# Fixing ScalarE's order in the stick-breaking attention of half 0

## The chip, the cores and the metric

The kernel runs on one core of a Trainium2 chip. A core has five engines with a queue each: TensorE (PE, with its weight loads as PEld), VectorE (DVE), ScalarE (ACT), GpSimd (POOL) and SyncE (SP), which issues nearly all DMAs here. Each engine takes its instructions strictly in order and waits on semaphores for the others. The metric is device time in microseconds for one execution, given as the median of several runs.

## The reference

A decoder layer of width 1024 on 2048 tokens and 16 meta tokens: an RMS norm, one wide input projection, stick-breaking attention (8 heads of 64), sliding-window attention with sinks (16 query heads), two gated branch projections, an output projection and a last norm. The change lies in the stick-breaking part:

```python
z = einsum('bqhd,bkhd->bhqk', q, k) * d ** -0.5
log_beta = log_sigmoid(z)
log_1m = where(mask, log_beta - z, 0.0)
rev = lax.cumsum(log_1m, axis=3, reverse=True)
suffix = concatenate([rev[..., 1:], zeros], axis=-1)
w = where(mask, exp(log_beta + suffix), 0.0)
out = einsum('bhqk,bkhd->bqhd', w, v)
```

With s = sigmoid(-z), the weight of a key is the product of s over all later keys, less that product with the key's own s in it. The kernel keeps the running product and multiplies it with differences of v.

## The kernel before

Tokens stand in reverse order, so the suffix product is a prefix product along a row. They are cut into four groups of 512 (16 blocks of 128); half 0 works on groups 2 and 3, half 1 on groups 0 and 1, and the meta tokens follow group 3 as keys. Matrix operands are split into a high and a low part, and a product is three matmuls (high by high, high by low, low by high).

In each half, projections and sliding-window attention come first, then stick-breaking attention, then more gate projections; a final stage does the branch and output projections. During stick-breaking TensorE alternates between gate projections (`gate`, whose matmuls are on L464 and whose result is taken out on L615) and attention steps. `weave` does that: for each piece of the main work it draws steps from the side generator `stick`, by a ratio of estimated costs.

`stick` goes over 8 heads, and in each over the half's query groups, group 3 first and then group 2. For a group it goes over n = 0 .. 3-g key groups and four rows j of each. A step s does the following.

- `row(h, g, n, j)` for step s: two score matmuls into one or two `ps_z` banks (L918), a sigmoid on ScalarE per bank (L921), and a scan on VectorE that forms the running product (L926 in the diagonal group, with the mask, L928 in the others). In the rows that reach the meta keys (the last n) GpSimd copies the 16 meta columns of the row into `mr` (L934).
- `turn` for the step six earlier (`LT[0]` is 6): up to four TensorE transposes into a `ps_t` bank (L943), then `evac_split`: ScalarE copies the bank out as `wth` (L126) and VectorE forms the remainder `wtl` (L127).
- When that earlier step is in the last key group and has i = 0, `split_meta`: ScalarE copies `mr` into the high half of `m` (L953, the meta copy), VectorE subtracts for the low half (L954, the remainder).
- When it has i = 1, `turn_meta`: TensorE transposes `m` (L959, the meta transpose) and ScalarE copies the result in four parts into `wm` (L963).
- `values` for a step before that: two matmuls with `wth` and `wtl` against v differences (L975); the last of a unit is the meta product with `wm`, after which four ScalarE instructions with a bias (L981) take the result out and DMAs store it.

A unit here is one head and one query group of half 0: 16 units, numbered in the order in which they run, each with one L953, one L954 and one L959. There are two banks each of `ps_g`, `ps_z`, `ps_t` and `ps_o`, 12 row buffers, and two buffers each of `mr` and `m`.

The order on TensorE is the program's own throughout (`manual_schedule` for PE at the top). For the other engines a scheduler of the framework places the instructions by a simulated timeline, except in stretches under `manual_schedule`: the start of the kernel (VectorE, ScalarE, SP) and the gate products after stick-breaking of half 0 (VectorE, ScalarE).

Of the kernel before, what the change touches and what calls it, by code (L numbers as in the profile page):

```python
# [48 lines left out]
def tile_kernel(ctx, tc, x, xt, meta, metat, gain, w_in, w_sb, w_sw, w_out, sinks, fgain,  # L49
# [94 lines left out]
    def weave(main, side, ratio, credit=0.0):  # L144

        for c in main:
            clock[0] += c
            credit = min(credit + c * ratio, 6.0)
            while credit > 0:
                n = next(side, None)  # L150
                if n is None:
                    credit = float("-inf")
                    break
                if n == 0:
                    credit = 0.0
                    break
                credit -= n
        return credit
# [5 lines left out]
    def drain(*gens):  # L164
        for _ in chain(*gens):
            pass
# [319 lines left out]
    def col_tile(w, g, use, first=False, bank="g", mbank="o"):  # L486

        acc = ps(bank)
        pm = None
        yield from gemm(acc, w, g, first)  # L490
        if first:
            pm = ps(mbank)
            gemm_meta(pm, w)
        use(g, acc, None if pm is None else meta_sum(pm))
        yield 0.65
# [125 lines left out]
    def tiles_by_tile(makes, groups, meta=False):  # L621
        for mk in makes:
            w, use, wants = mk()
            for n, g in enumerate(reversed(groups) if wants == "back" else groups):
                yield from lagged(col_tile(w, g, use, meta and wants and n == 0))
# [6 lines left out]
    def lagged(gen):  # L632

        for n, c in enumerate(gen):
            yield c
            if n in (2, 4, 6):
                flush({2: soon, 4: late, 6: pending}[n])
# [713 lines left out]
    for half, groups in enumerate(halves):  # L1351
# [61 lines left out]
        with tc.tile_pool(name=f"sb{half}", bufs=1, side="left") as bp:  # L1413
            hsplit[0] = vsplit[0] = False
            side = stick(groups, bp)
            drain(tiles_by_tile(gts[few:few + 1], groups))
            rest = 28 - FAST - PLAIN if half == 0 else 23
            cost_sb = 8 * sum(4 * (4 - g) for g in groups) * 1.31 + 16 * 0.33 + LT[half] * 0.86
            ratio = cost_sb / ((rest - few - 1) * 10.4)
            weave(tiles_by_tile(gts[few + 1:rest], groups), side, ratio)  # L1420
            if half == 0:
                hsplit[0] = vsplit[0] = True
                plain = [mk() for mk in gts[rest:rest + 2]]
            drain(side)
# [95 lines left out]
```

## Time and profile before

| | us |
|---|---|
| median of 3 runs | 2091.56 |
| lowest and highest run | 2090.66, 2092.18 |
| profiled execution | 2093.26 |
| its span, first to last instruction | 2091.4 |
| stick-breaking of half 0, from the span's start | about 372 to 562 |
| first and last L953 of half 0 | 380.46, 554.48 |

A profile row of a timeline gives start, duration, engine, line, operation, what it writes and reads, and in brackets the idle time of the engine just before it and the instruction that ended that. "Idle before" of a group is the sum over its instructions. A matmul row's duration contains its pipeline: matmuls of 512 columns that follow each other start about 0.23 us apart though each is given 0.39. So a delay of TensorE is read from starts, and from the idle time in brackets. PEclk is the clock that was granted to TensorE, 1.00 being full speed.

### The profile page before, as it was taken

The numbers are of one execution on the slowest core, as the hardware profiler recorded it, in microseconds if no ns is written. First come the engines' busy times: TensorE is split into PE (matmuls) and PEld (weight loads), VectorE is DVE, ScalarE is ACT, GpSimd is POOL, SyncE is SP. The second block draws the span as 40 slices with busy tenths as digits, with TensorE's granted clock in tenths as the row PEclk, the third lists the DMA queues.
The fourth block names the chain that finished last, engine by engine and source line by source line (L and its number), as shares of the span: only waits on it lengthen the run. The fifth ranks groups of instructions, "written<-read, shape, count | busy, mean of one in ns | idle before, by whom it ended". The sixth has DMA issues, their size and how long they took to land. (4 is left out here: it accounts for less than half of the span.)

```text
span 2091.4 us, 30949 instructions
## 1 busy us (share of the span) xinstructions
PE 2076.3 (99%) x10579; PEld 1744.8 (83%) x10579; DVE 1463.0 (70%) x2383; ACT 1091.4 (52%) x2657; POOL 345.7 (17%) x682
## 2 busy tenths in 40 slices
PE   9999999999999999999999999999999999999998
PEld 7888888888888888888888888888888888788887
DVE  7897986877687754887728788777774547464543
ACT  6677774577665335777735555655653212321121
POOL 1233444331000000233310000000000343000000
PEclk9999999999999999999999999999999999999999
DMA  9855555866377574435455344343424987568532
GB/s 338 307 195 201 188 175 179 252 199 185 91 278 298 209 247 163 159 126 177 150 171 161 120 130 129 114 129 98 121 83 165 350 318 223 182 229 305 154 100 91
DMA packets 170093, 391.46 MB, mean 187 GB/s; under 512 B 23728, under 2 KB 28208, under 8 KB 169936
## 3 DMA queue, kind: packets, MB, share of 16 engines
q1 hardware_dynamic: 169648, 389.23, 55.8%
q8 instruction: 83, 1.36, 0.3%
q14 instruction: 74, 0.61, 0.1%
q10 hardware_dynamic: 288, 0.27, 0.0%
HBM read 241.68 MB, written 145.18 MB: 185 GB/s over the span
## 5 line engine op out<-in xcount | busy, mean ns | idle before, releaser
L464 PE MATMUL ps_g<-xh,wh 128*128 128x512 f32 x1264 | 517.0, 409 | 1.1 <-DVE tmp L680 0.6
L464 PE MATMUL ps_g<-xl,wh 128*128 128x512 f32 x1264 | 495.6, 392 | 0.7 <-DVE xl L1199 0.6
L464 PE MATMUL ps_g<-xh,wl 128*128 128x512 f32 x1264 | 495.7, 392 | 0.0
L928 DVE TENSOR_TENSOR_SCAN row<-row 128x512 f32<-128x512 f32 (+4 forms) x256 | 290.1, 1134 | 116.2 <-POOL row L923 60.1
L464 PEld LDWEIGHTS ps_g<-xh,wl 128*128 128x128 f32 x1264 | 237.8, 188 | 52.7
L464 PEld LDWEIGHTS ps_g<-xh,wh 128*128 128x128 f32 x1264 | 238.5, 189 | 39.9 <-ACT xh L1198 1.4
L464 PEld LDWEIGHTS ps_g<-xl,wh 128*128 128x128 f32 x1264 | 239.2, 189 | 38.0 <-DVE xl L1199 1.8
L921 ACT ACTIVATE row<-ps_z 128x512 f32<-128x512 f32 (+4 forms) x352 | 175.1, 509 | 159.3 <-PE ps_z L918 155.0
L126 ACT ACTIVATE wth<-ps_t 128x512 fp32r<-128x512 f32 (+1 forms) x320 | 171.6, 536 | 61.4 <-PE ps_t L943 59.6
L127 DVE SCALAR_TENSOR_TENSOR wtl<-ps_t,wth 128x512 fp32r<-128x512 f32 (+1 forms) x320 | 188.7, 590 | 21.3 <-ACT wth L126 20.7
L918 PE MATMUL ps_z<-kt,q 128*128 128x512 f32 (+4 forms) x704 | 183.7, 349 | 2.0 <-ACT row L921 1.9
L943 PE MATMUL ps_t<-ident,row 128*128 128x128 f32 x1088 | 171.4, 273 | 1.0 <-DVE wtl L127 0.9
L943 PEld LDWEIGHTS ps_t<-ident,row 128*128 128x128 f32 x1088 | 134.5, 140 | 33.1 <-DVE wtl L127 1.8
L918 PEld LDWEIGHTS ps_z<-kt,q 128*128 128x128 f32 x704 | 124.4, 188 | 27.4 <-ACT row L921 5.1
L975 PE MATMUL ps_o<-wth,vc 128*128 128x512 f32 (+1 forms) x320 | 131.2, 410 | 0.0
L975 PE MATMUL ps_o<-wtl,vc 128*128 128x512 f32 (+1 forms) x320 | 116.4, 364 | 0.0
L767 ACT ACTIVATE sc<-sc,nm 128x129 f32<-128x129 f32 x256 | 100.0, 393 | 30.5 <-DVE nm L765 29.5
L934 POOL COPY mr<-row 128x16 f32<-128x16 f32 x128 | 28.4, 224 | 444.2 <-DVE row L928 401.8
L615 ACT ACTIVATE tmp<-ps_g 128x512 f32<-128x512 f32 x80 | 48.0, 600 | 80.5 <-PE ps_g L464 74.3
L299 ACT CAST ringl<-gt 128x512 fp32r<-128x512 f32 x32 | 19.9, 621 | 127.1 <-DVE gt L297 93.3
L117 POOL TENSOR_SCALAR wh<-raw 128x1024 fp32r<-128x1024 f32 (+1 forms) x45 | 49.8, 1108 | 212.7 <-PE ps_g L464 90.3
L123 POOL TENSOR_TENSOR wl<-raw,wh 128x256 fp32r<-128x256 f32 x88 | 83.2, 975 | 2.0
(442 smaller groups left out, 4202.3 us busy)
## 6 DMA issues: line engine op xcount, KB each, us to landing
wh<-h_in_w_in SPq DMA_DIRECT2D x66, 512.0 KB, 3.9
wl<-l_in_w_in SPq DMA_DIRECT2D x66, 512.0 KB, 5.1
h_in_w_in<-wh SPq DMA_DIRECT2D x50, 512.0 KB, 3.3
l_in_w_in<-wl SPq DMA_DIRECT2D x50, 512.0 KB, 4.1
raw<-in_w_in SPq DMA_DIRECT2D x49, 512.0 KB, 5.3
q<-qd SPq DMA_DIRECT2D x128, 128.0 KB, 3.2
vc<-vd SPq DMA_DIRECT2D x48, 256.0 KB, 3.2
kd<-tmp SPq DMA_DIRECT2D x32, 256.0 KB, 3.4
```

The costliest lines, as they stand in the source:

```text
L117: G.tensor_scalar(h, src, 1.0, 1.0, op0=ALU.mult, op1=ALU.mult)
L123: G.tensor_tensor(l[:, c], src[:, c], f32(h[:, c]), op=ALU.subtract)
L126: A.activation(h, acc, AF.Copy, scale=scale)
L127: V.scalar_tensor_tensor(l, acc, scale, f32(h), op0=ALU.mult, op1=ALU.subtract)
L464: T.matmul(acc, lhsT=a[:, k, :], rhs=b[:, k, :], start=k == i == 0, stop=k == KT - 1 and i == 2)
L615: A.activation(e, acc, AF.Sigmoid)
L767: A.activation(sc[:, hh, :], sc[:, hh, :], AF.Exp, bias=nm[:, hh:hh + 1], accum_out=den[:, hh:hh + 1])
L918: T.matmul(z[:, :m], lhsT=qt[:, j * P:(j + 1) * P], rhs=kt[h][:, k0 + c:k0 + c + m], start=t == 0, stop=t == 1)
L921: A.activation(r[:, c:c + m], z[:, :m], AF.Sigmoid, scale=-1.0)
L928: V.tensor_tensor_scan(r[:, :w], r[:, :w], r[:, :w], last[j] if n else 1.0, op0=ALU.mult, op1=ALU.min)
L943: T.transpose(tr[:, j * P:(j + 1) * P], rows_of[h, g, n - (j > i), j][:, k0:k0 + P], ident)
L975: T.matmul(o[:, :n], lhsT=v, rhs=r, start=first and r is wh, stop=last)
```

## The change

While `weave` runs in half 0, ScalarE too is under `manual_schedule`: its instructions stand in the order in which the program records them. GpSimd, VectorE and SP stay with the scheduler, whose timeline is worked out anew.

```diff
             ratio = cost_sb / ((rest - few - 1) * 10.4)
+            order = ExitStack()
+            if half == 0:
+                order.enter_context(tc.manual_schedule(engines={mybir.EngineType.Activation}))
             weave(tiles_by_tile(gts[few + 1:rest], groups), side, ratio)
+            order.close()
             if half == 0:
```

In the built kernels the instructions are the same in number and kind. ScalarE's order differs in the place of the 16 L953 alone, VectorE's in that of the 16 L954. Unit 1 on ScalarE, before and after:

```
before                          after
L921 row (last of the block)    L921 row (last of the block)
L953 m<-mr                      L921 row x3
L921 row x3                     L126 wth<-ps_t
L126 wth<-ps_t                  L615 tmp<-ps_g
L615 tmp<-ps_g                  L953 m<-mr
L921 row                        L921 row
L126 wth<-ps_t                  L126 wth<-ps_t
L963 wm<-ps_o x4                L963 wm<-ps_o x4
```

On VectorE L954 then stands directly behind the L127 that goes with the L126 in front of L953. TensorE's and GpSimd's orders are the same in both, and on SP two neighbouring DMAs have changed places.

## Prediction

> **What bounds the kernel now.** I read the page's busy line first, then the waits of the stage that the change touches, then the groups, then the timeline around single instructions.
>
> ```profile
> span 2091.4 us, 30949 instructions
> PE 2076.3 (99%) x10579; PEld 1744.8 (83%) x10579; DVE 1463.0 (70%) x2383; ACT 1091.4 (52%) x2657; POOL 345.7 (17%) x682
> ```
> TensorE is busy for all but 15.1 of 2091.4 us. So ScalarE's order is worth only what it adds to or takes from TensorE's waits. The half's stick-breaking runs from about 372 to 562 us. Its waits (engine and line that waited, what ended the wait, us in total, times, longest), then its busy times, then two groups (busy us, mean ns, idle time ahead):
>
> ```profile
> ACT m L953 <- POOL mr L934: 6.7, 8, 3.1
> DVE m L954 <- ACT m L953: 4.2, 6, 1.4
> PE ps_z L918 <- ACT row L921: 1.9, 3, 1.2
> ACT row L921 <- PE ps_z L918: 31.5, 60, 1.0
> 372.00:562.00 190.00, 187.62 (x1071) 158.95 (x1070) 149.16 (x213) 132.88 (x364) 42.23 (x89) 1.00 0.62 189
> L953 ACT CAST m<-mr 128x64 fp32r<-128x64 f32 x16 | 3.9, 243 | 6.9 <-POOL mr L934 6.7
> L959 PE MATMUL ps_o<-ident,m 128*128 128x128 f32 x16 | 4.3, 272 | 0.0
> ```
> ScalarE waits 6.7 us at the meta copy L953 and VectorE 4.2 us at the remainder L954 behind it. But TensorE idles only 190.00 - 187.62 = 2.4 us here, and never at the transpose L959, which reads what L953 and L954 wrote. TensorE's clock is 1.00 throughout.
>
> **The change, part by part.** No instruction is added or removed. There are 16 units (8 heads by 2 query groups), each with one L953, one L954 and one L959. The scheduler placed L953 just after the sigmoids of the row block that ends the unit; the program's own place is three steps later, behind the copy-out L126 of the transposes of `turn` with i = 0. L954 follows on VectorE, to just behind the L127 of the same transposes. In program order L959 is one step later on TensorE and does not move. Nothing else moves except one DMA pair on SP's queue: a gate result is now issued ahead of the low half of a weight copy.
>
> ```profile
> 493.33 0.38 SPq L59 DMA_DIRECT2D l_in_w_in<-wl  x1
> 493.83 0.35 SPq L59 DMA_DIRECT2D gs<-tmp  x1
> 494.23 1.08 SPq L59 DMA_DIRECT2D raw<-in_w_in  x1
> 500.07 0.32 SPq L59 DMA_DIRECT2D vc<-vd  x1
> ```
> In the trace SP issues these at 493.33 and 493.83, the load behind them at 494.23 for 1.08 us, and nothing until 500.07. Two issues that change places inside that row of issues cost nothing; the idle 4.8 us cover them, and without that cover it would be one issue, 0.4 us.
>
> **Unit 1** is the one with the long wait (start, us, engine, line):
>
> ```profile
> 379.63 0.39 PE L464 MATMUL ps_g<-xh,wl 128*128 128x512 f32 x1
> 380.46 0.24 ACT L953 CAST m<-mr 128x64 fp32r<-128x64 f32 x1 [3.13 <-POOL mr L934]
> 380.74 0.23 DVE L954 TENSOR_TENSOR m<-mr,m 128x64 fp32r<-128x64 f32 x1 [0.70 <-ACT m L953]
> 381.24 3.46 DVE L926 TENSOR_TENSOR_SCAN row<-row,mask 128x512 f32<-128x512 f32 x3 [0.27 <-ACT row L921]
> 381.25 0.73 PE L918 MATMUL ps_z<-kt,q 128*128 128x512 f32 x2 [1.24 <-ACT row L921]
> 382.96 0.62 PE L918 MATMUL ps_z<-kt,q 128*128 128x512 f32 x2
> 383.64 0.14 PEld L959 LDWEIGHTS ps_o<-ident,m 128*128 128x128 f32 x1
> 383.75 0.27 PE L959 MATMUL ps_o<-ident,m 128*128 128x128 f32 x1
> 384.61 0.67 DVE L127 SCALAR_TENSOR_TENSOR wtl<-ps_t,wth 128x512 fp32r<-128x512 f32 x1
> 385.19 1.21 DVE L926 TENSOR_TENSOR_SCAN row<-row,mask 128x512 f32<-128x512 f32 x1
> 385.33 0.20 PEld L943 LDWEIGHTS ps_t<-ident,row 128*128 128x128 f32 x2 [0.34 <-DVE wtl L127]
> ```
> Today L953 blocks the sigmoids behind it, so the score matmuls wait until 381.25. Without it they could follow the last gate matmul at 379.63 by about 0.23 (matmuls of 512 columns start that far apart): 1.4 us earlier, and 0.1 more because the held pair took 0.73 where a free one takes 0.62. TensorE would then come to L959 at 383.75 - 1.5 = 382.25. VectorE cannot follow so far. The scans before are done 0.70 + 0.23 + 0.27 = 1.2 us before 381.24, at 380.0. Three scans fill the 3.37 us from 381.24 to 384.61, so L127 starts at 380.0 + 3.37 = 383.37 and ends 0.67 later at 384.04. L954 is now behind it.
>
> The step from the end of L127 to L959: the next VectorE instruction starts 0.09 before L127's end (385.19 against 385.28), and L954 lasts 0.23: +0.14. TensorE takes up a result of VectorE 0.05 after its end (385.28 to 385.33). The matmul comes 0.11 behind its weight load (383.64 to 383.75). Together **0.30 us**. So L959 starts at 384.34: a wait of 2.1 us where there was none, and 0.59 later than today. The wait of 0.34 that today comes at 385.33 falls away, since it is for the same L127. Net for unit 1: 0.59 - 0.34 = **+0.25 us**; the gain of 1.5 is given back.
>
> On VectorE's instruction start there is a rule that can be left out of the sum. The Trainium skill, "VectorE: DVE Perf Modes", section "The DRAIN you can't avoid", says the next VectorE operation does not start until the pipeline is empty. By it L954 would begin at L127's end, 0.09 later in each of nine waits, and the total below would be 3.8 in place of 3.0. The rows at 384.61 and 385.19 show an earlier start, so I do not take it.
>
> **Units 2 to 16.** Here TensorE seldom waited, so its place at L959 stays what it is; the new wait is 0.30 plus the time by which L127 ends after that place. Units 2, 3, 8, 9, 14 and 16:
>
> ```profile
> 397.23 0.69 DVE L127 SCALAR_TENSOR_TENSOR wtl<-ps_t,wth 128x512 fp32r<-128x512 f32 x1 [0.42 <-ACT wth L126]
> 397.94 0.27 PE L959 MATMUL ps_o<-ident,m 128*128 128x128 f32 x1
> ...
> 405.51 0.67 DVE L127 SCALAR_TENSOR_TENSOR wtl<-ps_t,wth 128x512 fp32r<-128x512 f32 x1
> 405.93 0.27 PE L959 MATMUL ps_o<-ident,m 128*128 128x128 f32 x1
> ...
> 466.82 0.67 DVE L127 SCALAR_TENSOR_TENSOR wtl<-ps_t,wth 128x512 fp32r<-128x512 f32 x1
> 467.31 0.27 PE L959 MATMUL ps_o<-ident,m 128*128 128x128 f32 x1
> ...
> 474.89 0.66 DVE L127 SCALAR_TENSOR_TENSOR wtl<-ps_t,wth 128x512 fp32r<-128x512 f32 x1
> 475.99 0.27 PE L959 MATMUL ps_o<-ident,m 128*128 128x128 f32 x1
> ...
> 538.27 0.66 DVE L127 SCALAR_TENSOR_TENSOR wtl<-ps_t,wth 128x512 fp32r<-128x512 f32 x1
> 538.29 0.27 PE L959 MATMUL ps_o<-ident,m 128*128 128x128 f32 x1
> ...
> 558.31 1.37 DVE L127 SCALAR_TENSOR_TENSOR wtl<-ps_t,wth 128x512 fp32r<-128x512 f32 x2 [1.50 <-ACT wth L126]
> 558.86 0.27 PE L959 MATMUL ps_o<-ident,m 128*128 128x128 f32 x1
> ```
> Unit 2: L127 ends at 397.92, L959 at 397.94 is 0.02 after it, so a wait of 0.28. Unit 3: 406.18 against 405.93, 0.55. Unit 8: 0.48. Unit 14: 538.93 against 538.29, 0.94 (VectorE is late there from a weight split). Unit 16 (first of its two L127 ends at 559.00): 0.44. Unit 9: 475.55 leaves 0.44, no wait. Read the same way, units 4 and 12 give 0.26 each, 5 gives 0.39, 7 gives 0.03, and 6, 10, 11, 13 and 15 none. Sum 3.6; I take **3.3**, because in unit 5 VectorE's unbroken chain to that L127 starts with a wait for L953 that goes away, and most of its 0.39 with it.
>
> ScalarE's copy L953 itself (0.24) now stands between L126 and the next sigmoid. Queued behind it are that sigmoid, which TensorE needs two steps later, and the next L126. That sigmoid waits for its scores anyway (L921 waits for PE in 60 places of the stage), so I cost it at nothing; uncovered, it would be 0.24 a unit, 3.9 us in all.
>
> What goes away, besides unit 1: in units 10 and 12 L953 stood ahead of sigmoids that TensorE waited for.
>
> ```profile
> 486.08 0.40 PE L975 MATMUL ps_o<-wtl,vc 128*128 128x512 f32 x1
> 486.66 0.63 PE L918 MATMUL ps_z<-kt,q 128*128 128x400 f32 x2 [0.18 <-ACT row L921]
> ...
> 508.60 0.24 ACT L953 CAST m<-mr 128x64 fp32r<-128x64 f32 x1
> 508.73 1.15 ACT L981 ACTIVATE tmp<-ps_o,vf 128x128 f32<-128x128 f32 x4
> ```
> Unit 10: 0.58 from start to start where 0.23 is normal, 0.35 lost. Unit 12: ScalarE gets 0.13 (508.60 to 508.73) back out of a longer wait there that L981 makes. Together **-0.5 us**, and below 0.1 elsewhere. Sum: 0.25 + 3.3 - 0.55 = **+3.0 us**.
>
> The profiled execution took 2093.26 us, span 2091.4 and 1.9 around it; it stands 1.7 above the median of 2091.56. The sum makes that execution 2096.3 (span 2094.4). Set on the median: 2091.56 + 3.0 = 2094.6.
>
> Bounds. The step of 0.30 may be 0.20 (weight load hidden) or 0.45 (the 0.05 taken as 0.20): 2.5 to 4.8 for units 2 to 16. Unit 1 from -0.3 (VectorE starts its scans 0.5 sooner) to +0.8. Gains from 0.35 to 0.95 (unit 12's whole wait). That gives +1.2 to +5.3.
>
> **Rivals.**
> *The wait goes and no new one comes.* If L954 were done when TensorE reaches L959, as today in all 16 units, unit 1 would gain until the transposes at 385.33, which could start when L127 has ended at 384.04: 1.2, and with the 0.55 the time is 2089.8. For it: VectorE has idle time (149 of 190 us). Against it: L127, ahead of L954 in VectorE's queue, ends after L959's place in half of the rows above.
> *Slower by more than the forecast: each wait has a restart.* At 381.25 the pair behind the wait took 0.11 longer than a free one. If ten waits each cost that on top of the 0.30 (+1.1), and L954 began only at L127's end (+0.8), the sum is 3.0 + 1.9 = 4.9: 2096.5. It decides from 1.2 us more than my sum. For it: the 0.73 row. Against: the 0.11 is partly the weight load that is in the 0.30 already.
> *It does nothing:* units 2 to 16 wait less because each wait lets VectorE catch up, and the half's total is within 1 us: 2091.6. For it: VectorE is only 79% busy. Against: the lag in each unit is made within two steps, not carried.
>
> **How the numbers follow.** Forecast 0.5, restart 0.22, nothing 0.13, gain 0.1, else 0.05. I call 0.2% (4.2 us) about what a measurement of this kernel can tell from no change: below 2087.4 faster, above 2095.7 slower. The forecast's own range is +1.2 to +5.3, and a fifth of its chance lies above 4.2. Slower: 0.1 from the forecast and 0.15 of the restart's 0.22, 0.25. Faster: only the 0.05 of what I have not seen. Same: the rest, 0.70. The range reaches from just under the gain rival's side, 2090.0, to past the restart, 2098.0.
>
> **What would show it.** In the profile after, TensorE's wait of 1.24 at L918 near 381 is gone, and L959 has about nine waits for L954, in sum near 5 us with 2 in unit 1 and 0.9 in unit 14. ScalarE no longer waits at L953 for GpSimd. The time at which the stage ends moves by +3. I am wrong if L959 shows no waits (then the gain rival), or if TensorE waits at other lines.

## The result, and the profile after

| | before | after |
|---|---|---|
| median of 22 runs each, us | 2091.07 | 2094.26 |
| lowest and highest, us | 2089.27, 2093.0 | 2092.77, 2096.27 |
| profiled execution, us | 2093.26 | 2095.14 |
| first score matmul to last meta product of the stage, us | 373.5 to 563.3: 189.8 | 371.8 to 564.2: 192.4 |

The ratio is 1.0015, with a 95% interval from 1.0009 to 1.0021. So the changed kernel is 3.2 us slower. The interval leaves out 1, so the loss is measured, though its middle is below the 0.2% that the prediction called no change. The two profiled spans differ by 1.1 only. That is because the part before the stage, where the two programs are the same, took 1.7 less in the second profile (373.5 against 371.8). Over all the kernels profiled here, this start lies between 371.5 and 373.5. The length of the stage is therefore the figure to compare in the traces. It grew by 2.6 us, where the forecast said 3.0.

The page's busy line of the kernel after, then its waits in the stage (engine and line that waited, what ended the wait, us in total, times, longest):

```profile
span 2092.5 us, 30945 instructions
PE 2075.4 (99%) x10579; PEld 1742.7 (83%) x10579; DVE 1462.8 (70%) x2383; ACT 1091.0 (52%) x2657; POOL 346.2 (17%) x682
```

```profile
PEld ps_o L959 <- DVE m L954: 6.6, 10, 2.0
PE ps_o L959 <- DVE m L954: 3.8, 7, 1.7
ACT m L953 <- POOL mr L934: 1.1, 1, 1.1
PE ps_z L918 <- ACT row L921: 0.4, 1, 0.4
```
TensorE now waits at the meta transpose L959 for the remainder L954, a line at which it never waited before. Ten weight loads of L959 waited. In exchange, ScalarE's waits at the meta copy L953 fell from 6.7 us in 8 places to 1.1 in one, and TensorE's waits for sigmoids from 1.9 to 0.4. The windows view of the stage (us, then busy us of PE, PEld, DVE, ACT and POOL, then the clock) has the balance:

```profile
372.00:562.00 190.00, 185.78 (x1058) 156.72 (x1057) 147.07 (x210) 131.57 (x362) 42.08 (x89) 1.00 0.61 186
```
TensorE idles 4.2 us in this window, where it idled 2.4. That is 1.8 more by the rows, against 2.6 from start to start. A row's idle time begins at the modelled end of the matmul ahead, so it leaves out part of a short wait, and starts have to be compared.

Unit 1 after (start, us, engine, line):

```profile
377.44 4.27 DVE L926 TENSOR_TENSOR_SCAN row<-row,mask 128x144 f32<-128x144 f32 x4
378.00 3.71 POOL L934 COPY mr<-row 128x16 f32<-128x16 f32 x4
379.57 0.39 PE L464 MATMUL ps_g<-xh,wl 128*128 128x512 f32 x1
379.81 0.62 PE L918 MATMUL ps_z<-kt,q 128*128 128x512 f32 x2
380.26 0.49 PE L943 MATMUL ps_t<-ident,row 128*128 128x128 f32 x3
381.64 0.66 DVE L127 SCALAR_TENSOR_TENSOR wtl<-ps_t,wth 128x512 fp32r<-128x512 f32 x1
381.74 0.24 ACT L953 CAST m<-mr 128x64 fp32r<-128x64 f32 x1 [1.14 <-POOL mr L934]
382.22 0.21 DVE L954 TENSOR_TENSOR m<-mr,m 128x64 fp32r<-128x64 f32 x1
382.48 0.14 PEld L959 LDWEIGHTS ps_o<-ident,m 128*128 128x128 f32 x1 [1.97 <-DVE m L954]
382.49 0.33 PE L959 MATMUL ps_o<-ident,m 128*128 128x128 f32 x1 [1.73 <-DVE m L954]
383.84 0.38 PE L943 MATMUL ps_t<-ident,row 128*128 128x128 f32 x2
```
These are the rows of the forecast, in its order. The score pair follows the gate matmul at once (379.57 to 379.81) and takes 0.62. The scans fill VectorE until L127 at 381.64, and the instruction behind it, now L954, starts at 382.22, before L127 ends (382.30). L959 comes 0.05 after L954's end. It lost 1.9 us there, after a gain of 1.5 just ahead; the transposes L943 at 383.84 have no wait any more.

Other units after: 2 and 7, each with the GpSimd row beside L954, then 14.

```profile
396.19 2.27 POOL L123 TENSOR_TENSOR wl<-raw,wh 128x256 fp32r<-128x256 f32 x3
396.26 0.74 DVE L954 TENSOR_TENSOR m<-mr,m 128x64 fp32r<-128x64 f32 x1
...
451.16 1.04 POOL L117 TENSOR_SCALAR wh<-raw 128x1024 fp32r<-128x1024 f32 x1 [6.99 <-PE ps_g L464]
451.47 0.81 DVE L954 TENSOR_TENSOR m<-mr,m 128x64 fp32r<-128x64 f32 x1
452.33 0.33 PE L959 MATMUL ps_o<-ident,m 128*128 128x128 f32 x1 [0.26 <-DVE m L954]
...
537.96 0.66 DVE L127 SCALAR_TENSOR_TENSOR wtl<-ps_t,wth 128x512 fp32r<-128x512 f32 x1
538.54 0.21 DVE L954 TENSOR_TENSOR m<-mr,m 128x64 fp32r<-128x64 f32 x1
538.80 0.33 PE L959 MATMUL ps_o<-ident,m 128*128 128x128 f32 x1 [0.65 <-DVE m L954]
```
Unit 14 is the forecast's case: L954 is short, only late, behind an L127 that is late itself. Unit 7 is another. Its L954 took 0.81 us in place of 0.21 and ended just after GpSimd's instruction beside it (452.28 against 452.20). In unit 2 it took 0.74, beside GpSimd's weight split.

To see where the 2.6 us arose, I lined up the 16 meta products (L975 with `wm`), which exist in every kernel. The table gives the time of each since the stage's first score matmul, less the same time of the kernel before. The experiments stand in it too.

| shift in us after the meta product of unit | 1 | 2 | 4 | 6 | 7 | 9 | 10 | 13 | 14 | 16 |
|---|---|---|---|---|---|---|---|---|---|---|
| after | 0.1 | 1.3 | 1.5 | 1.9 | 1.4 | 1.8 | 1.3 | 1.4 | 2.2 | 2.6 |
| e1: transpose one step later | 0.1 | 0.0 | -0.2 | -0.3 | -0.7 | -1.0 | -1.6 | -2.1 | -2.2 | -1.9 |
| e2: copy one step earlier | -0.1 | -0.2 | -0.2 | -0.2 | -0.2 | -0.2 | -0.8 | -0.9 | -0.9 | -0.9 |
| e3: copy three steps earlier | 0.0 | 0.2 | 0.2 | 0.2 | 0.2 | 0.2 | 1.2 | 1.2 | 1.2 | 1.2 |
| e4: copy one step later | 3.3 | 9.5 | 13.4 | 18.0 | 17.5 | 21.0 | 25.1 | 28.6 | 32.2 | 33.2 |
| e5: before, transpose later | 0.2 | 0.1 | -0.1 | -0.1 | -0.6 | -0.9 | -0.7 | -1.1 | -1.1 | -0.9 |
| e6: remainder on GpSimd | 0.1 | 3.2 | 5.0 | 5.1 | 5.2 | 5.4 | 5.0 | 4.9 | 4.9 | 5.1 |
| e8: copy one, transpose two steps later | -1.2 | -1.3 | -1.5 | -1.5 | -1.9 | -2.2 | -2.8 | -3.3 | -3.4 | -3.3 |

The meta product of an even unit comes after the L959 of the next unit, so that unit's new wait shows under the even one: the 1.2 at unit 2 are the waits of units 2 and 3, the step before unit 6 is that of unit 7. The first row steps up there and at 14 and 16, and falls at 7 and 10.

### The profile page after: what moved, and what is told of

Read it like the earlier page. It is cut to its first block, busy times and chain, and to the rows that moved or that the text cites. A ratio compares the mean times of both kernels' runs of the same rounds, so it can differ in the third digit from the quotient of the medians.

```text
span 2092.5 us, 30945 instructions
## 1 busy us (share of the span) xinstructions
PE 2075.4 (99%) x10579; PEld 1742.7 (83%) x10579; DVE 1462.8 (70%) x2383; ACT 1091.0 (52%) x2657; POOL 346.2 (17%) x682
## 5 line engine op out<-in xcount | busy, mean ns | idle before, releaser
L127 DVE SCALAR_TENSOR_TENSOR wtl<-ps_t,wth 128x512 fp32r<-128x512 f32 (+1 forms) x320 | 188.7, 590 | 22.3 <-ACT wth L126 21.7
L126 ACT ACTIVATE wth<-ps_t 128x512 fp32r<-128x512 f32 (+1 forms) x320 | 171.6, 536 | 62.4 <-PE ps_t L943 59.8
L943 PE MATMUL ps_t<-ident,row 128*128 128x128 f32 x1088 | 171.3, 273 | 0.6 <-DVE wtl L127 0.6
L943 PEld LDWEIGHTS ps_t<-ident,row 128*128 128x128 f32 x1088 | 134.7, 140 | 32.1 <-DVE wtl L127 1.0
L975 PE MATMUL ps_o<-wth,vc 128*128 128x512 f32 (+1 forms) x320 | 131.2, 410 | 0.0
L975 PE MATMUL ps_o<-wtl,vc 128*128 128x512 f32 (+1 forms) x320 | 116.4, 364 | 0.0
L934 POOL COPY mr<-row 128x16 f32<-128x16 f32 x128 | 30.3, 238 | 445.5 <-DVE row L928 403.1
L117 POOL TENSOR_SCALAR wh<-raw 128x1024 fp32r<-128x1024 f32 (+1 forms) x45 | 50.5, 1123 | 211.7 <-PE ps_g L464 85.8
L926 DVE TENSOR_TENSOR_SCAN row<-row,mask 128x512 f32<-128x512 f32 (+2 forms) x64 | 69.6, 1095 | 22.5 <-ACT row L921 21.8
```

What stands on the lines that cost most here:

```text
L126: A.activation(h, acc, AF.Copy, scale=scale)
L127: V.scalar_tensor_tensor(l, acc, scale, f32(h), op0=ALU.mult, op1=ALU.subtract)
L926: V.tensor_tensor_scan(r[:, :w], r[:, :w], mask[:, :w], 1.0, op0=ALU.mult, op1=ALU.max)
L943: T.transpose(tr[:, j * P:(j + 1) * P], rows_of[h, g, n - (j > i), j][:, k0:k0 + P], ident)
L975: T.matmul(o[:, :n], lhsT=v, rhs=r, start=first and r is wh, stop=last)
```

## The experiments

The theory was that the loss is TensorE's wait at L959, because L954 is queued behind L127 on VectorE and L959 follows one step behind. The rivals were that the order of ScalarE itself costs (the copy standing in front of a sigmoid), or that the waits are hidden elsewhere and the loss is of another source.

### e1: give L954 one more step

TensorE's meta transpose is moved one step later in half 0; ScalarE's order stays as in the kernel after.

```diff
-                if g + step == 3 and i == 1:
+                if g + step == 3 and i == (2 if lt == 6 else 1):
                     turn_meta(h, g)
```


> The changed kernel with the meta transpose L959 one step later (at i = 2 in half 0); ScalarE's and VectorE's places of L953 and L954 stay as changed. Queue theory (TensorE's new waits come from L954 standing behind L127 on VectorE, just ahead of L959): a whole step of about 2 us now lies between, so L959 shows no waits, unit 1 keeps about 1.2 us and units 10 and 12 their 0.5: 1.7 us under the kernel before, ratio 0.9992. ScalarE theory (L953 costs because it now stands between L126 and the next sigmoid): nothing of that moved, so still about 3 us over the kernel before, ratio 1.0015.

Measured: 2089.47 against 2091.44 for the kernel before, ratio 0.9992 (0.9984 to 1.0001). TensorE no longer waits at L959 at all, and the stage went from +2.6 to -1.9. So without the wait at L959 the whole loss is gone, even with the 0.9 off that e5 below gives to the later transpose itself, and ScalarE's order does not cost. But the gain in unit 1 that I expected did not come (shift +0.1). The timeline of e1 at that place shows why:

```profile
379.51 3.71 POOL L934 COPY mr<-row 128x16 f32<-128x16 f32 x4
383.25 0.24 ACT L953 CAST m<-mr 128x64 fp32r<-128x64 f32 x1 [1.15 <-POOL mr L934]
383.40 0.59 ACT L921 ACTIVATE row<-ps_z 128x512 f32<-128x512 f32 x1
384.05 0.63 PE L918 MATMUL ps_z<-kt,q 128*128 128x272 f32 x3 [1.68 <-ACT row L921]
```
With no wait at L959, L953 itself is what is late. GpSimd's copies of the meta columns end at 383.22, ScalarE waits 1.15 for them with a sigmoid behind it, and TensorE waits 1.68 for that sigmoid. The late copy that the change removed from one place is waited for in another.

### e2, e3, e4: the copy at other places

L953 is issued one step earlier (e2), three steps earlier (e3, about where the scheduler had put it), or one step later, just ahead of the transpose (e4). ScalarE keeps the program's order in all three. In e2 `t + 1` stands where e3 has `t + 3`:

```diff
-                if g + step == 3 and i == 0:
+                if g + step == 3 and i == 0 and lt != 6:
                     split_meta(h, g)
...
+            h, g, step, i = steps[min(max(t + 3, 0), n - 1)]
+            if lt == 6 and 0 <= t + 3 < n and g + step == 3 and i == 0:
+                split_meta(h, g)
             while av_todo and turned[0] < s - 1:
```


> The changed kernel with split_meta one step earlier (behind the transposes of the step before), ScalarE still in program order. Queue theory: L954 stands behind the L127 of the step before, a step ahead of L959; no waits at L959 in units 2 to 16, unit 1 gains about 1.0, units 10 and 12 0.5: 1.5 us under the kernel before, ratio 0.9993. ScalarE theory: L953 still stands between an L126 and a sigmoid, so still about 3 us over, ratio 1.0015.

Measured: 2090.54 against 2091.44, ratio 0.9993 (0.9984 to 1.0002). The waits in the stage of e2:

```profile
ACT m L953 <- POOL mr L934: 2.4, 1, 2.4
PE ps_o L959 <- DVE m L954: 0.6, 1, 0.6
```
Nine of the ten waits are gone without TensorE's order being touched. Only unit 1 still waits, again for GpSimd, and it gained 0.1 where I had expected 1.0. The stage is 3.5 shorter than in the kernel after.

> ScalarE in program order as in the changed kernel, but split_meta called three steps earlier, which puts L953 and L954 within one or two instructions of where the scheduler had them. Queue theory: only the place matters, so the kernel before again, within 0.5 us, ratio 1.0000, with the 1.2 us wait at L918 in unit 1 back. Rival (an order written by hand costs by itself, or the pair of DMAs or another stage): 3 us over, ratio 1.0015.

Measured: 2092.83, ratio 1.0007 (0.9999 to 1.0016). The stage is 1.2 longer than before, where no more than 0.5 was expected, and 1.0 of it arises in unit 10. Its timeline:

```profile
484.38 0.25 ACT L953 CAST m<-mr 128x64 fp32r<-128x64 f32 x1 [2.07 <-POOL mr L934]
484.53 1.14 ACT L981 ACTIVATE tmp<-ps_o,vf 128x128 f32<-128x128 f32 x4
486.00 0.63 PE L918 MATMUL ps_z<-kt,q 128*128 128x400 f32 x2 [1.21 <-ACT row L921]
```
In e3 L953 stands ahead of the four L981 there, and everything behind it on ScalarE waits 2.07 for GpSimd. In four of the 16 units L953 stands two to five instructions off the scheduler's place. So this run is near the kernel before, but not a copy of its order. It shows what one wrong place costs.

For e4 the copy is one step later:

```diff
-                if g + step == 3 and i == 0:
+                if g + step == 3 and i == (1 if lt == 6 else 0):
                     split_meta(h, g)
```


> The changed kernel with split_meta one step later, just ahead of turn_meta: L953 and L954 stand behind L126 and L127 of the transposes next to L959. Queue theory: in each of 16 units L959 waits for L126 (0.5 to 0.6), L127 (0.5 to 0.7) and 0.3 more, 1.3 to 1.6 less up to 0.7 of other matmuls in between: 14 to 26 us in all, about 20 over the kernel before, ratio 1.0095. ScalarE theory: one L953 a unit between an L126 and a sigmoid as in the changed kernel, so about 3 us over, ratio 1.0015.

Measured: 2125.65, ratio 1.0162 (1.0148 to 1.0176): 34 us slower, above the range that I gave. The waits of e4 in the stage:

```profile
PEld ps_o L959 <- DVE m L954: 33.4, 16, 3.6
PE ps_o L959 <- DVE m L954: 26.9, 15, 3.3
```
All 16 units wait now, about 2.1 us each at the weight load. This is the same chain as in the kernel after, with the L126 and L127 of the very step ahead of the copy in the two queues.

### e5 and e7: which part of e1's gain is the order

e5 is the kernel before with e1's edit alone. e7 has e1's edit and ScalarE's order in both halves.

> Control: the kernel before (ScalarE left to the scheduler) with only the transpose L959 one step later in half 0. Queue theory: L959 had no wait before, so nothing to gain: ratio 1.0000, within 0.5 us, and the 1.2 us wait at L918 in unit 1 stays; the 0.9992 of the changed kernel with the later transpose needs both edits. Rival (a later transpose is worth about 2 us by itself): 0.9992 here too.

Measured: 2090.57 against 2090.87, ratio 0.9997 (0.9989 to 1.0006). The stage is 0.9 shorter than before, where at most 0.5 was expected, and its waits are still those of the scheduler's order:

```profile
ACT m L953 <- POOL mr L934: 7.8, 9, 3.1
PE ps_z L918 <- ACT row L921: 2.5, 4, 1.2
```
By the traces, 0.9 of e1's 1.9 us is the later transpose by itself and 1.0 is the order, nearly all of it between units 9 and 13 (there e1 falls by 1.1 and e5 by 0.2). By the timed runs the two are not told apart.

> Both edits (ScalarE's program order while the woven part of stick-breaking runs, transpose L959 at i = 2) in half 1 too. In half 1 of the kernel before ScalarE waits 4.1 us at L953 in 6 places, and TensorE has one larger wait, 0.7 us. Queue theory: half 1 gains at most that 0.7, so 1.7 to 2.4 us under the kernel before, ratio 0.9990. ScalarE theory: 3 us over in each half, ratio 1.003.

Measured: 2089.97 against 2090.87, ratio 0.9995 (0.9986 to 1.0004). Half 0 gains 1.9 in the trace, as in e1. Half 1 gains nothing: set on the same start, its shift against the kernel before is -2.74 us at its first meta product and -2.75 at its last. The expected gain there did not exist.

### e6: take L954 out of VectorE's queue

```diff
-            V.tensor_tensor(m[:, :, 1], st["mr"], f32(m[:, :, 0]), op=ALU.subtract)
+            (G if lt == 6 else V).tensor_tensor(m[:, :, 1], st["mr"], f32(m[:, :, 0]), op=ALU.subtract)
```


> The changed kernel with the remainder L954 of half 0 computed on GpSimd in place of VectorE; L953 keeps its changed place on ScalarE, L959 its own. VectorE theory (what is late is VectorE's queue in front of L954, not L953): in units 1, 3 and 14, where VectorE ran behind, the wait at L959 falls from 2.0, 0.5 and 0.9 to 0.6 or less, so the total is 0 to 2 us under the kernel before, ratio 0.9991 to 1.0000, except where GpSimd itself is in a weight split (L117, L123, up to 6.7 us) as the unit comes: each such unit adds up to 5 us. ScalarE theory (L953 comes too late behind L126): waits at L959 as in the changed kernel, ratio 1.0015.

Measured: 2099.06 against 2090.87, ratio 1.0036 (1.0023 to 1.005). The profiled spans differ by 5.8 us (2097.2 against 2091.4), and the stage makes 5.1 of them. The rest of the 8.2 is that the profiled execution of the kernel before stood 2.4 above the median used here (2093.26 against 2090.87). Where GpSimd was free, the waits of units 3, 7, 14 and 16 are gone, with L953 at the same place; where GpSimd was splitting weights, they are longer. Unit 2 and then unit 14 in e6:

```profile
397.80 2.91 POOL L123 TENSOR_TENSOR wl<-raw,wh 128x256 fp32r<-128x256 f32 x4
400.67 0.31 POOL L954 TENSOR_TENSOR m<-mr,m 128x64 fp32r<-128x64 f32 x1
401.04 0.33 PE L959 MATMUL ps_o<-ident,m 128*128 128x128 f32 x1 [2.98 <-POOL m L954]
...
542.29 0.47 POOL L954 TENSOR_TENSOR m<-mr,m 128x64 fp32r<-128x64 f32 x1 [0.79 <-ACT m L953]
543.14 0.27 PE L959 MATMUL ps_o<-ident,m 128*128 128x128 f32 x1
```
In unit 14 L954 waits for ScalarE alone and L959 for nobody. So in units 3, 7, 14 and 16 VectorE's queue, and not L953 on ScalarE, was late in the kernel after. Unit 1 is different: there TensorE still waits 1.67 us, where 0.6 or less was expected, because L953 itself comes late, after 1.12 us of waiting for GpSimd's copies. The price is the same kind of wait in another queue: L954 behind four pieces of L123.

### e8: the copy when it is ready, the transpose two steps behind it

e1 left unit 1 waiting for GpSimd's copies, so L953 has to come later there; and L959 then needs its two steps.

```diff
-                if g + step == 3 and i == 0:
+                if g + step == 3 and i == (1 if lt == 6 else 0):
                     split_meta(h, g)
-                if g + step == 3 and i == 1:
+                if g + step == 3 and i == (3 if lt == 6 else 1):
                     turn_meta(h, g)
```


> The changed kernel with the meta copy L953 and remainder L954 one step later (i = 1) and the meta transpose L959 two steps later (i = 3) in half 0. The queue theory, with what the kernel of e1 showed in unit 1 (L953 waited 1.15 us for GpSimd's copies L934, which ran beside VectorE's scans at 1.1 us each, and the score matmuls behind it waited 1.7): L953 now comes after those copies, so unit 1 waits only for the L127 of its first transposes, 1.2 us better than with the transpose later alone; no waits at L959; 2.9 us under the kernel before, ratio 0.9986. ScalarE theory (an L953 between L126 and a sigmoid costs): still 3 us over, 1.0015. If GpSimd's copies do not matter in unit 1: 0.9992 as with the transpose later alone.

Measured: 2087.58 against 2090.66, ratio 0.9984 (0.9975 to 0.9993). It is faster than both kernels, by 3.1 us against the one before, and the stage is 3.3 shorter. The windows view of e8, then its timeline in unit 1:

```profile
372.00:562.00 190.00, 189.35 (x1085) 162.17 (x1084) 153.11 (x219) 134.37 (x371) 44.36 (x89) 1.00 0.62 189
```

```profile
381.32 0.63 PE L918 MATMUL ps_z<-kt,q 128*128 128x272 f32 x3 [0.27 <-ACT row L921]
381.93 0.24 ACT L953 CAST m<-mr 128x64 fp32r<-128x64 f32 x1 [0.28 <-POOL mr L934]
382.55 0.20 PEld L943 LDWEIGHTS ps_t<-ident,row 128*128 128x128 f32 x2 [0.34 <-DVE wtl L127]
```
TensorE idles 0.65 us in the window, against 2.4 before and 4.2 after. L953 waits 0.28 for GpSimd in unit 1 in place of 1.15, TensorE 0.27 for the sigmoid in place of 1.68, and the unit gains the 1.2 that e1 had not shown (first column of the table). From unit 2 on the row of e8 runs beside that of e1, some 1.2 to 1.4 lower.

## Why the prediction was right

The mechanism was right, and so was the sum: +3.0 forecast, +3.2 in the medians, +2.6 in the stage. That the sum came so close is partly luck, as two misses cancelled. Point by point:

- **Unit 1: forecast +0.25, measured about +0.1.** TensorE came 1.5 earlier to L959, as said, and then lost 1.9 there; the 0.34 at the transposes behind it fell away to within 0.05. With the times set back on those of the kernel before, whose stage starts 1.67 later, L959 starts at 384.16, forecast 384.34, and L127 ends at 383.97, forecast 384.04.
- **The handover step: 0.19 where I took 0.30.** L954 starts 0.08 before L127's end and lasts 0.21 (forecast 0.09 and 0.23), and the weight load follows its end by 0.05. But the matmul starts 0.01 behind its weight load (382.48, 382.49), not 0.11: this was the lower bound given. From L127's end at 382.30 that makes 0.19, and in unit 14, from 538.62, 0.18. The row at 382.22 also bears on the rule weighed from the Trainium skill, "VectorE: DVE Perf Modes", section "The DRAIN you can't avoid". The prediction gave only half of it: the section goes on, "A next op that is not held starts earlier". L954, which started 0.08 before L127's end, agrees with that half.
- **Units 2 to 16: net right, terms mis-sized.** From start to start, the steps at L959 were 0.70 in unit 2 (forecast 0.28), 0.44 in 3 (0.55), 0.14 in 4 (0.26), 0.42 in 7 (0.03), 0.36 in 8 (0.48), 0.81 in 14 (0.94) and 0.33 in 16 (0.44), with 5 and 12 below 0.2. The big misses are units 2 and 7. There the price of L954 was mis-sized. I took 0.23 for every one, from the kernel before, but at its new place it runs beside GpSimd's weight split and takes 0.74 and 0.81. The other terms came out about 0.1 lower each, which is the handover's 0.11, and this made up for it. With the 1.90 of unit 1 all new waits come to 5.2, where "near 5" was forecast. Behind each of the ten waits the next matmul came another 0.05 or 0.06 later, since L959 took 0.33 us in place of 0.27. The sum had no term for that. With it, units 2 to 16 lost about 3.9 where I took 3.3.
- **Gains of -0.55: unit 10 gave 0.45 (forecast 0.35) and unit 12 0.15 (0.13).** One was missed: 0.44 came back in unit 7, at transposes that waited 0.27 for L127 in the kernel before and found VectorE done in the kernel after. Part of the forecast's rival "it does nothing" was thus true: a wait lets VectorE catch up. With a few smaller ones the gains come to 1.3. This miss of 0.8 and the 0.6 too little on the waits nearly cancel, which nothing in the working foresaw.
- **L953 at its new place and the DMA pair: nothing, as costed.** e1 keeps both and is not slower than the kernel before.
- **After the stage**, 0.4 was lost near 610, where ScalarE waited longer for a DMA that the change does not touch. I can't say that it belongs to the change.

Of the rivals, e1 tested "the wait goes and no new one comes", since there L959 does not wait. The total is near the 2089.8 given, but not for the reason given: its 1.2 from unit 1 was not there, as GpSimd's copies come next. This shows what my working left out. I had traced unit 1 through VectorE only, while in the kernel after L953 waits 1.14 for GpSimd and is done at 381.98, only 0.3 before L127. With VectorE free, L959 would by these rows have gained no more than those 0.3. The sign that ScalarE would no longer wait at L953 failed in this unit, too. "Restart" was true only in the 0.06 behind each wait, where it had 0.11: L954 did not wait for L127's end, and the clock stayed at 1.00. And the argument that L127 ends after L959's place in half of the rows shown was too low a count: it is four of six.

What stays open: the 0.7 us by which e6's profile is longer outside the stage, and the split of e1's gain between the two edits, which only the traces tell.

## What to carry to other kernels

An engine that is idle half the time can still hold up the one that sets the time, through what is queued behind its waiting instruction. So for each short instruction between two engines, look both ways: what it waits for (too early, and it blocks its queue) and who reads it (too late, and the reader waits). Whoever fixes the place of one such instruction has to look at the place of its reader with it: the copy and the transpose moved together gained 3 us, the copy alone cost 3 or 34 us at two places, and at a third, one step earlier (e2), it cost nothing that could be measured. And a moved instruction is priced at its new place, beside what runs there, not by its mean from the old.

## What the runs showed of the hardware

**VectorE and GpSimd can slow each other.** The line view of GpSimd's copies L934 in unit 1, first before, then after (duration in ns: least, median, most):

```profile
L934 POOL COPY mr<-row x4: 192/193/360, 379.7 to 380.2; 128x16 f32<-128x16 f32 x4
```

```profile
L934 POOL COPY mr<-row x4: 360/1171/1177, 378.0 to 380.5; 128x16 f32<-128x16 f32 x4
```
A copy of 16 columns took 0.19 us where VectorE's scans were nearly done, and 1.17 beside the scans at 377.44 (four in 4.27 us, 1.07 each): about one scan for one copy. L954 in unit 7 is the same the other way round, ending 0.08 after GpSimd's L117. Not every overlap costs L954: in unit 5 it started at 428.85, 0.01 behind an L123 of GpSimd, and took 0.21, while that L123 took 0.82. The Trainium skill, "SBUF — State Buffer", section "Who interferes with whom", says that a VectorE instruction with two inputs in SBUF contends with a GpSimd instruction that reads SBUF, that the ports they share are an exclusive lock, and that the order of issue decides who is blocked. These rows agree with the contention: the scan reads `row` and `mask`, and L954 reads `mr` and `m`. Which of the two issued first in unit 5 they do not show.

**TensorE's clock fell to half after a wait of 2.2 us, but not after another.** In e4, unit 11 in the timeline, then three windows:

```profile
521.69 0.48 PE L959 MATMUL ps_o<-ident,m 128*128 128x128 f32 x1 [2.20 <-DVE m L954]
522.39 0.63 PE L975 MATMUL ps_o<-wtl,vc 128*128 128x512 f32 x1
522.82 0.63 PE L464 MATMUL ps_g<-xh,wh 128*128 128x512 f32 x1
```

```profile
522.00:524.00 2.00, 2.00 (x6) 1.61 (x6) 0.00 (x0) 1.03 (x4) 0.00 (x0) 0.50 0.00 0
524.00:526.00 2.00, 2.00 (x11) 1.72 (x11) 0.00 (x0) 1.24 (x5) 0.00 (x0) 0.78 0.50 139
414.00:416.00 2.00, 2.00 (x13) 1.74 (x13) 0.00 (x0) 1.44 (x6) 0.00 (x0) 1.00 0.19 28
```
After the wait of 2.20 the clock is 0.50 and matmuls of 512 columns start 0.43 apart in place of 0.23. After a wait of 2.19 in unit 3 (the window at 414) it stayed at 1.00. The clock of e4's stage is 0.50 in three stretches of 3.413 us, from 384.94, 402.01 and 521.48. These starts are 5 and 35 times 3.413 apart. Cut into stretches of that length from there, the trace has 2.6, 2.0 and 2.0 us of idle TensorE in the three stretches just ahead of these, and at most 1.7 in any other of the stage. So in this run it was the idle time within one such stretch that went with the loss, and not the length of the wait: the 2.66 of unit 7 fell into two. Against the kernel after, TensorE's starts lose about 1.5 us in each of the three, some 4.5 of e4's 34 us. The Trainium skill, "TensorE: Matmul & The Clock Gate", section "🎯 Why this matters for your kernels", asks for no gap of TensorE over about 3 us; here 2.20 went with a lost clock in one unit, and 2.19 did not in another.
